# Attention scores' maxima written to SBUF, filler paced by the share of attention work done, and one more gate pair in the quad stage

## The chip, the cores and the metric

The kernel runs on one core of one Trainium2 chip. The metric is device time in microseconds, as the median of the runs. A core has five engines that work side by side from their own queues: TensorE (PE, matrix products), VectorE (DVE), ScalarE (ACT), GpSimd (POOL) and SyncE (SP, which here only issues transfers). PE writes its results to the accumulator memory (PSUM), from which DVE and ACT read; all else lives in SBUF or in device memory.

## The reference

One layer of a streaming encoder, on a prompt of 1024 rows and a sample of 64 rows, all of width 1024 and in float32. One input projection gives nine groups of columns:

```python
xn = rms_norm(x, g_pre)
z = xn @ w_in
xa, ga, q, k, v, gb, fl, ma, mb = jnp.split(z, np.cumsum(sizes)[:-1], axis=-1)
```

Branch A is a causal convolution and a gated linear recurrence over `xa`, times silu(`ga`). Branch B is softmax attention with 16 heads of 64, whose logits carry running sums of log forget gates:

```python
s = jnp.einsum('qhd,khd->hqk', q, k) * (HEAD_DIM ** -0.5)
s = s + cq.T[:, :, None] - ck.T[:, None, :]
s = jnp.where(mask[None], s, -jnp.inf)
p = jax.nn.softmax(s, axis=-1)
return jnp.einsum('hqk,khd->qhd', p, v)
```

times silu(`gb`). Each branch is projected, weighted by sigmoid(`ma`) or sigmoid(`mb`), and the sum goes through one output projection, a norm, the residual and a small gated projection of a per-layer input. The sample attends to a cache of 128 keys beside its own.

## The kernel before, in words

All matrix operands are split in a high and a low part (`xh`, `xl`, `wh`, `wl`), and each product is made of three matmuls: high by high, high by low, low by high. The sequence of the stages is: the projection of `v` (to 123 us), two plain gate panels (to 147 us), the quad stage (to 411 us), attention (to 849 us), branch A's recurrence with its own panels (to about 1030 us), the branch projections, the output projection, and the last gated projection.

**Panels and quads.** A panel is 128 columns of `w_in` times all 1088 rows of `x`: three chunks of 364, 364 and 360 rows, eight steps of `k` each, three matmuls a step (`panel_steps`, L172 to L174; 72 matmuls). A quad is a pair of such panels made by seven half-size products instead of eight (`seven`, `product`, L818): 7 products of 4 `k` steps, 3 matmuls, 2 halves of 272 rows; 168 matmuls. The list `quads` holds the keys and queries, then `xa` and early `ga` columns, then `MORE` pairs of gate columns that are taken from the end of the list `gates`. What is left in `gates` are the panels that serve as filler in attention. The results of gate panels and quads are parked in device memory (`d_ma`, `d_mb`, `d_gb`, `d_ga`).

**Attention.** A unit is one head and one block of 256 queries (64 units, in the order of blocks 0, 3, 1, 2 in each head). Its steps are: `s`, the scores of 128 queries into one of two accumulator tiles, `s1` (up to 512 keys) or `s2` (up to 1024), one of each; `softmax`, which on DVE adds the mask and takes the row's maximum (L1143), on ACT takes the exponential with row sums (L1145), on DVE the reciprocal (L1147) and on POOL the normalisation (L1148) of the SBUF tile `pr` (named `pb` or `pm` in the trace); `t`, three or four transposes of `pr` on PE (L1185), whose result ACT and DVE split in `th` and `tl` (L83, L86); and `v`, four matmuls with the values (L1213, L1215), which end with a copy `lo` on ACT and a sum `y` on DVE. The sample's steps are `sk`, `ss`, `st` and `sv`. POOL makes the values' high and low halves `vv` (L1109, L86) from transfers that SP issues (`load_v`).

**What sets the order.** The order on PE, ACT, DVE and POOL in attention is written by a planner while the kernel is built. It keeps a clock `now` that moves by the cost of each matmul group, and `book` puts the work of the other engines in their calendars at the costs of the constants at the top (`D_MAX`, `A_EXP`, `G_NORM` and so on). `ready` tells when the next step of each of the three queues may start by this calendar: for `s`, when the accumulator tile is free (`s_free`); for `t`, when both normalisations and a transpose tile are done; for `v`, when `tl` is. The main loop takes the first queue whose step has been ready for `SLACK` = 600 ns; if there is none it takes one filler step (3 matmuls of a gate panel), and only when there is no filler left does it wait for the earliest step. A finished filler chunk is copied out of the accumulator by ACT (`st`); the weights of the next filler panel are split on ACT and DVE (`book_split`). The transfers for head 0 and its values are issued when the stage begins.

After attention, `recur_in(1)` takes the first panel of branch A (72 matmuls, beginning at L172 with the tag `acc`), while ACT and DVE make the convolution of the first 128 channels, which the matmuls `gacc` need after 96 further matmuls. `split_next` splits the next panel with two copies on ACT (`wh`, `wl`) and an adding transfer.

Of the kernel before, what the change touches and what calls it, by code (L numbers as in the profile page):

```python
# [9 lines left out]
AF = mybir.ActivationFunctionType  # L10
ALU = mybir.AluOpType
# [3 lines left out]
D = 1024  # L15
KT = D // P
# [10 lines left out]
NEG = -1e30  # L27
# [5 lines left out]
CW = HT // 2  # L33
PLAIN = 2

MORE = 2
W_SC = 1092
GC = 364

HOP_PE, HOP, SLACK = 250.0, 90.0, 600.0  # L40
D_MAX, D_INV, D_LO, D_Y, D_YS = (310.0, 1.035), 160.0, (130.0, 1.1), 420.0, 230.0
A_EXP, A_HI, A_LO, A_ST, A_W = (450.0, 0.85), (150.0, 0.88), 380.0, 470.0, 1060.0
G_NORM = (260.0, 0.84)
# [23 lines left out]
def hybrid_step(tc, a, o):  # L67
# [939 lines left out]
    def book(engine, at, ns, do=None):  # L1007

        busy = booked[engine]
        while busy and busy[0][1] < now[0] - 20000.0:  # L1010
            busy.pop(0)
        i = 0
        while i < len(busy) and busy[i][0] < at + ns:
            at = max(at, busy[i][1])
            i += 1
        busy.insert(i, (at, at + ns))
        if do is not None:
            serial[0] += 1
            heapq.heappush(agenda, (at, serial[0], do))
        return at + ns + HOP  # L1020
# [6 lines left out]
    def per(cost, n):  # L1027
        return cost[0] + cost[1] * n
# [67 lines left out]
    def load_v(p, i, tag="v_raw"):  # L1096

        raw = p2.tile([P, SEQ if tag == "pb" else SEQ // 2], F32, name=tag, tag=tag, bufs=4 if tag == "pb" else 1)
        raw = raw[:, :SEQ // 2].rearrange("q (b d) -> q b d", d=P)
        b = slice(4 * i, 4 * i + 4)  # L1100
        sp.dma_start(raw, o["v_prompt"][i * SEQ // 2:(i + 1) * SEQ // 2, p * P:(p + 1) * P].rearrange(
            "(b q) d -> q b d", q=P))
        for j in range(2):
            if i == 0:
                heads_v[2 * p + j] = p2.tile([P, NBLK, 2, HD], F32R, name="vv", tag="vv", bufs=3)
            vv = heads_v[2 * p + j]
            src = raw[:, :, j * HD:(j + 1) * HD]
            at = now[0] + 8000.0 + 3000.0 * j
            at = book("G", at, 360.0, lambda vv=vv, src=src: pool.tensor_copy(vv[:, b, 0, :], src))  # L1109

            def low(vv=vv, src=src):
                sub(pool, vv[:, b, 1, :], src, f(vv[:, b, 0, :]))
                n_halves[0] += p == 0

            book("G", at, 740.0, low)
# [6 lines left out]
    def load_sample(p):  # L1122
        cols = slice(p * P, (p + 1) * P)
        t = {n: p2.tile(s, F32, name=n, tag=n, bufs=1) for n, s in (("kc", [P, P]), ("vc", [P, P]), ("vn", [DEC, P]))}
        sp.dma_start(t["kc"][:, :], a["cache_k"][:, cols])
        sp.dma_start(t["vc"][:, :], a["cache_v"][:, cols])
        sp.dma_start(t["vn"][:, :], o["v_sample"][:, cols])
        sp.dma_start(f(cs_k[2:, :]), d_cs[2 * p:2 * p + 2].rearrange("h s t -> (h s) t"))
        sp.dma_start(f(cs_q[:2, :]).rearrange("s (h t) -> s h t", h=2), d_cq[:, 2 * p:2 * p + 2, :])
        t["ks"] = [p2.tile([P, LS], F32R, name=f"ks{i}", tag=f"ks{i}", bufs=1) for i in "hl"]  # L1130
        for i in range(2):
            sp.dma_start(f(t["ks"][i][:, PAST:]), d_k[i, p][:, SEQ:])
            for j in range(2):
                js = slice(j * HD, (j + 1) * HD)
                sp.dma_start(f(qs[i][js, js]), d_q[i, p][js, SEQ:])
        smp[p] = t
        smp_at[p] = now[0] + (12000.0 if p else 24000.0)

    def softmax(s, n, pr, m):


        nm, sm = (p2.tile([P, 1], F32, name=x, tag=x, bufs=8)[:, :] for x in ("nm", "sm"))
        at = book("D", now[0] + HOP_PE, per(D_MAX, n), lambda: dve.tensor_tensor_reduce(  # L1143
            out=s[:, :n], in0=s[:, :n], in1=m, scale=-1.0, scalar=-NEG, op0=ALU.add, op1=ALU.min, accum_out=nm))
        free = book("A", at, per(A_EXP, n), lambda: act.activation(  # L1145
            out=pr[:, :n], in_=s[:, :n], func=AF.Exp, scale=-1.0, bias=nm, accum_out=sm))
        at = book("D", free, D_INV, lambda: dve.reciprocal(out=sm, in_=sm))  # L1147
        return free, book("G", at, per(G_NORM, n), lambda: pool.tensor_scalar(  # L1148
            out=pr[:, :n], in0=pr[:, :n], scalar1=sm, scalar2=1.0, op0=ALU.mult, op1=ALU.mult))

# [216 lines left out]
    load_v(0, 0)  # L1367
    load_v(0, 1, "pb")
    load_sample(0)
    fill = filler()  # L1370
    while s_q or t_q or v_q:
        catch_up()
        times = [(i, ready(q[0])) for i, q in enumerate((s_q, t_q, v_q)) if q]
        times = [(i, at) for i, at in times if at is not None]
        best = next((i for i, at in times if at + SLACK <= now[0]), None)
        if best is None:
            if next(fill, False):
                continue
            at, best = min((at, i) for i, at in times)
            now[0] = max(now[0], at)  # L1380
            catch_up()
        go((s_q, t_q, v_q)[best].popleft())
    while next(fill, False):
        catch_up()
    catch_up(float("inf"))
# [872 lines left out]
```

## Time and profile before

| what | us |
|---|---|
| median of 3 runs (lowest, highest) | 1454.27 (1453.98, 1455.23) |
| the profiled execution, whole | 1453.95 |
| its span, first to last instruction | 1452.0 |
| around the span | 1.95 |
| PE busy | 1429.0 |
| DVE, ACT, POOL busy | 898.5, 715.5, 317.3 |

In the profile a matmul's row shows its start and a modelled length that overlaps the next one's: matmuls of 364 columns start 0.166 us apart and are shown as 0.33 us long. So what a group of matmuls costs is read from the starts of the first and of the row behind the last, and a wait of PE costs the shown idle time and the part of the length that would have overlapped, some 0.16 us more.

### The profile page before, as it was taken

The page shows a single profiled execution, that of the slowest core. Times are in us where ns is not written, and L with a number is a line of the kernel's source. Part 1 is how long each engine was busy: PE and PEld are TensorE (multiplying, and loading weights), DVE is VectorE, ACT ScalarE, POOL GpSimd, SP SyncE. Part 2 cuts the span into 40 slices and gives each one's busy share as a digit, 9 for nine tenths or more (in the row PEclk, how much of TensorE's full clock was granted, in tenths as well). Part 3 has the DMA queues.
Part 4 walks back from the last instruction along what each step waited for, and adds up shares of the span by engine and source line. Part 5 has one row for each costly group of instructions (what it writes and reads, how often), then busy time and mean ns, then how long its engine had stood idle before and what let it go on. Part 6 is the DMA issues. An engine that isn't in the chain of part 4 may idle for free.

```text
span 1452.0 us, 25721 instructions
## 1 busy us (share of the span) xinstructions
PE 1429.0 (98%) x9653; PEld 1388.6 (96%) x9653; DVE 898.5 (62%) x1640; ACT 715.5 (49%) x1353; POOL 317.3 (22%) x449
## 2 busy tenths in 40 slices
PE   8999999999999999999999999999999999999997
PEld 8999999999999999999999989999999999879997
DVE  5554765664325666666566555898747565788544
ACT  5423534442225566666555656777535233554533
POOL 0012333323223443444333310221011000000001
PEclk9999999999999999999999999999999999999999
DMA  6767556754276665646545344454178775134101
GB/s 220 214 129 109 150 159 176 189 181 114 83 204 162 121 148 140 139 115 140 124 128 137 57 109 73 89 94 83 65 264 306 264 216 176 58 107 157 48 34 44
DMA packets 143544, 200.64 MB, mean 138 GB/s; under 512 B 24212, under 2 KB 106620, under 8 KB 142396
## 3 DMA queue, kind: packets, MB, share of 16 engines
q1 hardware_dynamic: 126316, 162.61, 43.5%
q0 software_dynamic: 6336, 19.67, 4.9%
q10 hardware_dynamic: 10768, 16.73, 3.2%
q8 instruction: 76, 1.25, 0.3%
q14 instruction: 48, 0.39, 0.1%
HBM read 131.04 MB, written 65.80 MB: 136 GB/s over the span
## 4 chain that ended last, share of the span: by engine, by line
PE 82%; DVE 7%; DMA 4%; ACT 3%; issue 2%; POOL 1%; SPq 0%; DVEq 0%; ACTq 0%; POOLq 0%
PE quad L818 17%; PE acc L174 11%; PE acc L172 11%; PE acc L173 11%; PE tp L1185 4%; PE q L1905 4%; PE pv L1213 2%; PE pv L1215 2%; PE s L1163 2%; PE s L1164 2%; PE vacc L172 2%; PE vacc L173 1%; PE vacc L174 1%; DMA d_mix<-st_a 1%; DMA d_y<-y 1%
## 5 line engine op out<-in xcount | busy, mean ns | idle before, releaser
L172 PE MATMUL acc<-xh,wh 128*128 128x364 f32 (+1 forms) x768 | 252.5, 329 | 0.2 <-ACT st L83 0.2
L173 PE MATMUL acc<-xl,wh 128*128 128x364 f32 (+1 forms) x768 | 251.6, 328 | 0.0
L174 PE MATMUL acc<-xh,wl 128*128 128x364 f32 (+1 forms) x768 | 251.4, 327 | 0.0
L172 PEld LDWEIGHTS acc<-xh,wh 128*128 128x128 f32 x768 | 144.5, 188 | 1.2 <-ACT st L83 0.5
L173 PEld LDWEIGHTS acc<-xl,wh 128*128 128x128 f32 x768 | 144.3, 188 | 0.5
L174 PEld LDWEIGHTS acc<-xh,wl 128*128 128x128 f32 x768 | 144.1, 188 | 0.0
L1143 DVE CUSTOM_DVE_ANT_0 s<-s,mask 128x1024 f32<-128x1024 f32 (+7 forms) x128 | 95.5, 767 | 30.0 <-PE s L1164 29.7
L86 DVE TENSOR_TENSOR wl<-w_raw,wh 128x1024 fp32r<-128x1024 f32 (+1 forms) x53 | 60.1, 1135 | 71.5 <-ACT wh L83 68.1
L83 ACT ACTIVATE wh<-w_raw 128x1024 fp32r<-128x1024 f32 (+1 forms) x65 | 63.3, 975 | 82.9 <-PE quad L818 30.0
L1148 POOL TENSOR_SCALAR pb<-pb,sm 128x896 f32<-128x896 f32 (+1 forms) x64 | 61.7, 963 | 139.9 <-DVE sm L1147 120.3
L86 DVE TENSOR_TENSOR tl<-tp,th 128x512 fp32r<-128x512 f32 x96 | 65.8, 689 | 29.2 <-ACT th L83 29.1
L818 PE MATMUL quad<-xh,wh 128*128 128x272 f32 x384 | 80.7, 291 | 0.0
L818 PE MATMUL quad<-xl,wh 128*128 128x272 f32 x384 | 79.5, 288 | 0.0
L818 PE MATMUL quad<-xh,wl 128*128 128x272 f32 x384 | 79.4, 288 | 0.0
L83 ACT ACTIVATE th<-tp 128x512 fp32r<-128x512 f32 x96 | 57.0, 597 | 37.8 <-PE tp L1185 37.5
L1145 ACT ACTIVATE pb<-s,nm 128x896 f32<-128x896 f32 (+1 forms) x64 | 61.1, 955 | 26.0 <-DVE nm L1143 25.1
L1163 PE MATMUL s<-k,q 128*128 128x256 f32 (+1 forms) x192 | 67.1, 353 | 0.2 <-ACT pb L1145 0.2
L1164 PE MATMUL s<-k,q 68*128 68x256 f32 (+1 forms) x192 | 65.0, 350 | 0.0
L1185 PE MATMUL tp<-ident,pb 128*128 128x128 f32 x416 | 63.7, 274 | 1.2 <-DVE diag0l L86 0.7
L173 PE MATMUL acc<-ybl,wh 128*128 128x364 f32 (+1 forms) x192 | 62.9, 328 | 0.0
L174 PE MATMUL acc<-ybh,wl 128*128 128x364 f32 (+1 forms) x192 | 62.8, 327 | 0.0
L172 PE MATMUL acc<-ybh,wh 128*128 128x364 f32 (+1 forms) x192 | 62.6, 326 | 0.0
(718 smaller groups left out, 4167.4 us busy)
## 6 DMA issues: line engine op xcount, KB each, us to landing
w_raw<-in_w_in SPq DMA_DIRECT2D x56, 256.0 KB
q<-d_q SPq DMA_DIRECT2D x48, 256.0 KB
k<-d_k SPq DMA_DIRECT2D x48, 256.0 KB
w_raw<-in_w_in SPq DMA_DIRECT2D x64, 128.0 KB
w_raw<-in_w_branch SPq DMA_DIRECT2D x32, 256.0 KB
wl<-w_raw POOLq DMA_DIRECT2D x12, 512.0 KB, 4.6
wraw<-in_w_in SPq DMA_DIRECT2D x20, 256.0 KB
d_k<-oh ACTq DMA_DIRECT2D x16, 272.0 KB
```

The costliest lines, as they stand in the source:

```text
L83: return act.activation(out=out, in_=in_, func=AF.Copy, scale=scale)
L86: return eng.tensor_tensor(out=out, in0=in0, in1=in1, op=ALU.subtract)
L172: pe.matmul(out, ah, bh, start=start, stop=False)
L173: pe.matmul(out, ah, bl, start=False, stop=False)
L174: pe.matmul(out, al, bh, start=False, stop=stop)
L818: pe.matmul(acc[:, c, :CW], l[:, k, :], r[:, k, c * CW:(c + 1) * CW], start=(first and k == 0 and p == 0), stop=(k == 3 and p == 2), skip_ ...
L1143: at = book("D", now[0] + HOP_PE, per(D_MAX, n), lambda: dve.tensor_tensor_reduce(out=s[:, :n], in0=s[:, :n], in1=m, scale=-1.0, scalar=-N ...
L1145: free = book("A", at, per(A_EXP, n), lambda: act.activation(out=pr[:, :n], in_=s[:, :n], func=AF.Exp, scale=-1.0, bias=nm, accum_out=sm))
L1148: return free, book("G", at, per(G_NORM, n), lambda: pool.tensor_scalar(out=pr[:, :n], in0=pr[:, :n], scalar1=sm, scalar2=1.0, op0=ALU.mul ...
L1163: pe.matmul(s[:, c0:c0 + w], t["q1"][:, q0:q0 + P], t["k1"][:, c0:c0 + w], start=True, stop=False)
L1164: pe.matmul(s[:, c0:c0 + w], t["q2"][:HD + 4, q0:q0 + P], t["k2"][:HD + 4, c0:c0 + w], start=False, stop=True)
L1185: pe.transpose(tp[:, o0 + i * P:o0 + (i + 1) * P], pr[par][:, kb * P:(kb + 1) * P], ident[:, :])
```

## The change

Four things are changed.

1. `softmax` writes the masked scores into the SBUF tile `pr` instead of back into the accumulator tile, and the exponential runs in place in `pr`. The accumulator tile counts as free when DVE has taken the maximum, no longer when ACT has taken the exponential.
2. The main loop counts the attention work done so far (`own`, by `own_time`) and the filler steps used (`filled`). Where the next step isn't ready for 600 ns, filler is taken only up to the same share of filler as of own work; beyond it, the step that is ready first goes ahead if it has been ready for `LEAST` = 300 ns.
3. The first head's value halves are booked on POOL 20 us after the stage begins, no longer 8 us.
4. `MORE` is 3: one more pair of `gb` panels (columns 256 to 511) is made as a quad, and attention has 360 filler steps instead of 408.

```diff
-MORE = 2
+MORE = 3
...
-HOP_PE, HOP, SLACK = 250.0, 90.0, 600.0
+HOP_PE, HOP, SLACK, LEAST = 250.0, 90.0, 600.0, 300.0
...
-            at = now[0] + 8000.0 + 3000.0 * j
+            at = now[0] + (8000.0 if p else 20000.0) + 3000.0 * j
...
         at = book("D", now[0] + HOP_PE, per(D_MAX, n), lambda: dve.tensor_tensor_reduce(
-            out=s[:, :n], in0=s[:, :n], in1=m, scale=-1.0, scalar=-NEG, op0=ALU.add, op1=ALU.min, accum_out=nm))
-        free = book("A", at, per(A_EXP, n), lambda: act.activation(
-            out=pr[:, :n], in_=s[:, :n], func=AF.Exp, scale=-1.0, bias=nm, accum_out=sm))
-        at = book("D", free, D_INV, lambda: dve.reciprocal(out=sm, in_=sm))
+            out=pr[:, :n], in0=s[:, :n], in1=m, scale=-1.0, scalar=-NEG, op0=ALU.add, op1=ALU.min, accum_out=nm))
+        free = at
+        at = book("A", at, per(A_EXP, n), lambda: act.activation(
+            out=pr[:, :n], in_=pr[:, :n], func=AF.Exp, scale=-1.0, bias=nm, accum_out=sm))
+        at = book("D", at, D_INV, lambda: dve.reciprocal(out=sm, in_=sm))
...
+    def own_time(step):
+
+        kind, x, i = step
+        if kind == "s":
+            full = 256 * (units[x][1] + 1)
+            return sum(2 * (0.44 * min(512, full - c0) + 8) for c0 in range(0, full, 512))
+        if kind == "t":
+            return 109.0 * (3 if i == units[x][1] else 4)
+        return {"v": 480.0, "sk": 109.0, "ss": 440.0, "st": 218.0, "sv": 840.0}[kind]
+
     fill = filler()
+    own_total = sum(own_time(step) for q in (s_q, t_q, v_q) for step in q)
+    own = 0.0
+    filled = 0
+    n_fill = 3 * KT * (1 + sum(e[0][0] == "r" for e in ahead) + sum(len(g[1]) for g in gates))
     while s_q or t_q or v_q:
         catch_up()
         times = [(i, ready(q[0])) for i, q in enumerate((s_q, t_q, v_q)) if q]
         times = [(i, at) for i, at in times if at is not None]
         best = next((i for i, at in times if at + SLACK <= now[0]), None)
         if best is None:
-            if next(fill, False):
+            at, first_ = min((at, i) for i, at in times) if times else (now[0] + 1e9, None)
+            over = filled >= n_fill * own / own_total
+            if not (over and at + LEAST <= now[0]) and next(fill, False):
+                filled += 1
                 continue
-            at, best = min((at, i) for i, at in times)
+            best = first_
             now[0] = max(now[0], at)
             catch_up()
-        go((s_q, t_q, v_q)[best].popleft())
+        step = (s_q, t_q, v_q)[best].popleft()
+        own += own_time(step)
+        go(step)
```

How the planner's order moves is seen at three places. Lines of the changed kernel behind the softmax are one higher than before (L1186 is the transposes' line).

**POOL, where attention begins.** `vv` are the first head's value halves, made from the transferred `v_raw` and `pb`; `pm` and `pb` with `sm` are the normalisations of the first units. Before:

```order
L1109 CAST vv<-v_raw 128x4x64
L86 TENSOR_TENSOR vv<-v_raw,vv 128x4x64
L1109 CAST vv<-pb 128x4x64
L86 TENSOR_TENSOR vv<-pb,vv 128x4x64
L1088 DMA d_ma<-st 128x364
L1148 TENSOR_SCALAR pm<-pm,sm 128x128
L1088 DMA d_ma<-st 128x364
L1148 TENSOR_SCALAR pb<-pb,sm 128x896
L1148 TENSOR_SCALAR pm<-pm,sm 128x256
```

Of the change:

```order
L86 TENSOR_TENSOR vv<-v_raw,vv 128x4x64
L1109 CAST vv<-pb 128x4x64
L86 TENSOR_TENSOR vv<-pb,vv 128x4x64
L1149 TENSOR_SCALAR pm<-pm,sm 128x128
L1109 CAST vv<-v_raw 128x4x64
L86 TENSOR_TENSOR vv<-v_raw,vv 128x4x64
L1109 CAST vv<-pb 128x4x64
L86 TENSOR_TENSOR vv<-pb,vv 128x4x64
L1149 TENSOR_SCALAR pb<-pb,sm 128x896
L1149 TENSOR_SCALAR pm<-pm,sm 128x256
```

The first normalisation now stands between the halves of the first and of the second head, no longer behind both, and no filler's outgoing transfer stands between the normalisations.

**PE, at the end of attention.** Before, from the last filler row on, there are scores, transposes and value products alone, down to the first matmul of branch A. Its last rows:

```order
L1185 MATMUL tp_10560<-ident,pb 128x128 x3
L1213 MATMUL pv<-tl,vv 128x256
L1215 MATMUL pv<-th,vv 128x256
L1213 MATMUL pv<-tl,vv 128x256
L1215 MATMUL pv<-th,vv 128x256
L1213 MATMUL pv<-tl,vv 128x256
L1215 MATMUL pv<-th,vv 128x256
L1213 MATMUL pv<-tl,vv 128x256
L1215 MATMUL pv<-th,vv 128x256
L1213 MATMUL pv<-diag0l,vv 128x256
L1215 MATMUL pv<-diag0h,vv 128x256
```

Of the change, with the semaphores that each row waits for; the last row is the first matmul of branch A:

```order
L1216 MATMUL pv<-th,vv 128x256
L172 MATMUL acc<-xh_110,wh 128x360
L173 MATMUL acc<-xl_112,wh 128x360
L174 MATMUL acc<-xh_110,wl 128x360
L1214 MATMUL pv<-diag0l,vv 128x256 [waits DVE_49]
L1216 MATMUL pv<-diag0h,vv 128x256
L1214 MATMUL pv<-diag0l,vv 128x256
L1216 MATMUL pv<-diag0h,vv 128x256
L172 MATMUL acc<-xh_109,wh 128x364 [waits Activation_49]
```

Filler rows stand between the last units down to the last four matmuls of attention, and the first matmul of branch A waits for ACT, which it did not before. What it waits for is the copy `st` of the filler's last chunk, whose accumulator bank it takes.

**ACT, at the same place.** `wh` and `wl` from `w_raw` are the split of branch A's second panel, `st` is that last filler copy, `lo` the last unit's copy, `g_h` and `uh` belong to branch A. Before, `wh`, `st` and `wl` stand some twenty rows earlier, among the last units' exponentials, and the stage ends with:

```order
L83 ACTIVATE lo<-pv 64x256 [waits DVE_49,PE_49]
L83 ACTIVATE th<-tp_10531 128x512 [waits PE_49]
L83 ACTIVATE th<-tp_10545 128x512 [waits DVE_49,PE_49]
L83 ACTIVATE lo<-pv 64x256 [waits DVE_49,PE_49]
L83 ACTIVATE diag0h<-tp_10560 128x384 [waits PE_49]
L83 ACTIVATE lo<-pv 64x256 [waits DVE_49,PE_49]
```

Of the change:

```order
L83 ACTIVATE lo<-pv 64x256 [waits DVE_49,PE_49]
L83 ACTIVATE diag0h<-tp_10596 128x384 [waits PE_49]
L83 ACTIVATE wh<-w_raw 128x1024 [waits DMAHW2_49,DMAHW1_49,DMAHW7_49,DMAHW0_49,PE_49]
L83 ACTIVATE st<-acc 128x360 [waits DMASW5_49,PE_49]
L83 ACTIVATE lo<-pv 64x256 [waits DVE_49,PE_49]
L83 ACTIVATE wl<-wh 128x1024 [waits Activation_49]
L83 ACTIVATE g_h<-st 128x256 [waits DMAHW5_49,DMAHW3_49,DMAHW6_49,DMAHW2_49,Pool_49]
```

The split of the second panel now stands ahead of the copy that branch A's first matmul waits for.

## The prediction

> **What bounds the kernel now.** I read the page's list of engines first, then busy times by stage, then PE's waits and its timeline where the waits lie.
>
> ```profile
> PE 1429.0 (98%) x9653; PEld 1388.6 (96%) x9653; DVE 898.5 (62%) x1640; ACT 715.5 (49%) x1353; POOL 317.3 (22%) x449
> ```
>
> PE is busy for 98% of the span, so a change is worth only what it takes from PE's work or from its few waits. By stage (columns: length, then busy time and instructions of PE, PE's weight loads, DVE, ACT, POOL; granted clock, transfer share, GB/s):
>
> ```profile
> 146.87:390.42 243.55, 243.55 (x1949) 242.62 (x1949) 144.98 (x217) 95.38 (x176) 78.08 (x58) 1.00 0.53 151
> 390.42:411.50 21.08, 21.08 (x171) 21.08 (x170) 6.08 (x8) 2.89 (x5) 6.36 (x15) 1.00 0.69 209
> 411.50:831.86 420.36, 418.57 (x2820) 403.07 (x2819) 253.52 (x650) 240.72 (x566) 159.46 (x245) 1.00 0.58 132
> 831.86:849.05 17.19, 13.80 (x95) 11.48 (x95) 10.42 (x23) 11.45 (x23) 4.60 (x10) 1.00 0.58 119
> ```
>
> The first two are eleven quads and the last one, without a gap on PE. The third is attention as long as there is filler: 1.79 us idle in 420. The fourth is the end of attention, after the last filler row, and there PE stands idle for 3.39 us of 17.19. DVE and ACT are busy for 57 to 60% of attention, so neither is the bound. PE's waits, first from 440 to 831.8 us and then from 831.8 to 849.1 us:
>
> ```profile
> PE pv L1213 <- ACT lo L83: 0.4, 2, 0.2
> ```
>
> ```profile
> PE tp L1185 <- DVE tl L86: 1.2, 2, 0.8
> PE tp L1185 <- DVE diag0l L86: 0.7, 1, 0.7
> PE pv L1213 <- DVE y L1224: 0.6, 1, 0.6
> PE pv L1213 <- ACT lo L83: 0.5, 1, 0.5
> PE s L1163 <- ACT pb L1145: 0.2, 1, 0.2
> ```
>
> While filler lasts, two waits of 0.2 us are all that 390 us show. Without it, the short chain score, maximum, exponential, normalisation, transpose, split, values is laid bare.
>
> **The pair as a quad.** PE's timeline at the last quad, at the first filler panel, and at one more place:
>
> ```profile
> 390.42 0.41 PE L818 MATMUL quad<-xh,wh 128*128 128x272 f32 x2
> ...
> 411.50 0.33 PE L172 MATMUL acc<-xh,wh 128*128 128x364 f32 x1
> ...
> 423.40 0.33 PE L172 MATMUL acc<-xh,wh 128*128 128x364 f32 x1
> ...
> 437.49 0.32 PE L174 MATMUL acc<-xh,wl 128*128 128x360 f32 x1
> 439.14 0.55 PE L1185 MATMUL tp<-ident,pm 128*128 128x128 f32 x3 [1.34 <-POOL pm L1148]
> ```
>
> From 411.50 to 423.40 runs one panel of 72 matmuls: 11.90 us, two of them 23.80. The last quad, a gate pair too, takes 21.08 (390.42 to 411.50). The thirteenth costs the same, and its sums and splits lie beside PE (DVE 6.08 and ACT 2.89 of 21.08). So this gives -2.72. If it cost the mean of the eleven, 243.55/11 = 22.14 with the keys' transposes, which a gate pair doesn't have, it would give -1.66; I take -2.72, by the row that is of its kind. Its weights are now loaded in the place of `w_raw`, and the first filler's load waits behind their split; but on SP that load already stands behind the quad's last results, so nothing is later.
>
> **The first value halves.** The wait at 439.14 is POOL's. POOL's timeline:
>
> ```profile
> 431.20 0.40 POOL L1109 CAST vv<-v_raw 128x256 fp32r<-128x256 f32 x1 [24.95 <-DMA v_raw<-out_v_prompt]
> ...
> 436.65 0.39 POOL L1148 TENSOR_SCALAR pm<-pm,sm 128x128 f32<-128x128 f32 x1
> ```
>
> The halves stand ahead of the normalisations in the queue, although their data lands only at 431.2, and four pairs of them keep POOL until 436.65. In the new order the first normalisation follows the second pair, the other two follow the fourth, and two outgoing transfers are gone from ahead of and between them. So they end sooner, and the wait goes: 439.14 - 437.49 - 0.16 = 1.49 us (bounds -1.49, and 0 if the transposes should move forward by as much). Values aren't needed before the transposes, so the later halves delay nothing.
>
> **Filler to the end.** What would the end of attention cost without waits? Counts and pace:
>
> ```profile
> L1185 PE MATMUL tp<-ident,pb 128*128 128x128 f32 x26 | 4.2, 279 | 1.2 <-DVE diag0l L86 0.7 <-DVE tl L86 0.4
> L1185 PE MATMUL tp<-ident,pm 128*128 128x128 f32 x10 | 1.6, 274 | 0.8 <-DVE tl L86 0.8
> L1163 PE MATMUL s<-k,q 128*128 128x512 f32 x3 | 1.3, 428 | 0.2 <-ACT pb L1145 0.2
> L1163 PE MATMUL s<-k,q 128*128 128x256 f32 x2 | 0.6, 283 | 0.0
> ```
>
> ```profile
> 833.04 0.49 PE L1185 MATMUL tp<-ident,pm 128*128 128x128 f32 x3
> ...
> 833.84 0.60 PE L1185 MATMUL tp<-ident,pb 128*128 128x128 f32 x4
> ...
> 834.63 0.28 PE L1215 MATMUL pv<-diag2h,vv 128*128 128x256 f32 x1
> ```
>
> The first three score pairs (512, 256 and 512 keys) run from 831.86 to 833.04, 1.18 us; the other two (512 and 256) then take 1.18 x 768/1280 = 0.71. Three transposes with four value matmuls take 0.80, four with four 0.91 (833.84 to 834.63, and 0.12 for the last). There are 36 transposes (six groups of four, four of three), five score pairs, and, of the 95 matmuls, 95 - 1 - 36 - 10 = 48 for values, two groups of four without transposes. Work: 6 x 0.91 + 4 x 0.80 + 2 x 0.48 + 1.18 + 0.71 = 11.5. The stretch takes 17.19, so its waits cost 5.7; I enter -5.6. The lower bound is the shown idle time with 0.16 for each of the six listed waits: 4.4. The new order keeps filler between the units down to the last four matmuls, so each of these steps finds its data older.
>
> **A new wait.** The last filler chunk is now finished 0.65 us ahead of the end of attention (three matmuls' last at 0.166, then four of 0.12), and its copy `st` stands on ACT behind the split `wh`. What that pair takes is shown where it stood before:
>
> ```profile
> 831.90 1.06 ACT L83 ACTIVATE wh<-w_raw 128x1024 fp32r<-128x1024 f32 x1 [1.17 <-PE acc L173]
> 832.86 0.45 ACT L83 ACTIVATE st<-acc 128x360 f32<-128x360 f32 x1
> ```
>
> From the start of `wh` to the end of `st` it is 1.41 us. `wh` starts when L173, the last matmul but one, has ended (0.33 us after its start, which is 0.65 + 0.166 ahead of the end), some 0.45 us ahead of the end, so branch A's first matmul waits 1.0 us, and all of PE's queue behind it. Bounds: 0 (if `wh` waited less) and 1.4. The matmuls `gacc` stand 96 places behind; their operands come later too, since the last `lo` is late and two small loads now stand ahead of the convolution's input on SP:
>
> ```profile
> 832.12 1.13 SPq L1426 DMA_DIRECT2D st<-in_w_rg_a  x2
> ```
>
> ```profile
> 861.07 1.30 DVE L86 TENSOR_TENSOR ul<-u,uh 128x1092 fp32r<-128x1092 f32 x1 [0.85 <-ACT uh L83]
> ```
>
> ```profile
> 864.97 0.33 PE L172 MATMUL gacc<-uh,g_h 128*128 128x364 f32 x1
> ```
>
> `ul` ends at 862.37, so 2.6 us are spare; 1.13 for the loads and about 0.5 for `lo` fit in. If that cover were gone, each microsecond over would be one on PE.
>
> **The softmax and the thinner slack.** The accumulator tile is free one exponential sooner, which lets scores be placed earlier; it removes no work. Prices of the pieces in attention:
>
> ```profile
> L1143 DVE CUSTOM_DVE_ANT_0 s<-s,mask 128x1024 f32<-128x1024 f32 x16 | 19.7, 1230 | 7.4 <-PE s L1164 7.4
> ```
>
> ```profile
> L1145 ACT ACTIVATE pb<-s,nm 128x1024 f32<-128x1024 f32 x16 | 17.9, 1116 | 2.4 <-DVE nm L1143 1.7 <-DVE sm L1147 0.7
> ```
>
> and in the quad stage, ACT's copies of one size from SBUF (`ko`) and from the accumulator (`quad`):
>
> ```profile
> L83 ACT ACTIVATE oh<-ko 128x544 fp32r<-128x544 f32 x32 | 20.9, 654 | 16.9 <-DVE ko L849 16.6
> L83 ACT ACTIVATE ko<-quad 128x544 f32<-128x544 f32 x12 | 7.3, 611 | 0.0
> ```
>
> The planner's price for the maximum at 1024, 310 + 1.035 x 1024 = 1370, covers the measured 1230 and the reading of the result behind it; for the exponential, 450 + 0.85 x 1024 = 1320 stands over 1116. So 300 ns of its slack are about 300 real ones. The maximum has the same operands and writes elsewhere; the trace shows no such form, and I take no difference (40 ns either way, as ACT's pair differs, is off PE's path). The exponential from SBUF may cost 654 - 611 = 43 ns more, 136 times 5.8 us of ACT, which has 180 us idle; it makes normalised rows 43 ns later against 300 of slack. I take 0 for it, with 5.8 as the price if every one were exposed.
>
> [...]
>
> Steps that now go ahead at 300 ns, not 600, may meet late data. In the bare end of attention six waits cost 5.6, 0.9 each; I enter one such, +0.9 (bounds 0, and 3.7 for four).
>
> **The sum**, against the profiled execution (1453.95; the span is 1452.0): -2.72 - 1.49 - 5.6 + 1.0 + 0.9 = -7.9, so 1446.0. The median of the runs shown stands 0.32 above the profiled one: 1446.4. The likeliest case's own range is 1444.5 (neither of the two costs) to 1448.6 (the smaller gains of quad and end).
>
> **Rivals.** *All covers hold*: no wait at branch A, none from thin slack: -9.8, so 1444.5. For it speaks the quiet middle of the stage; against it ACT's order, `wh` ahead of `st`. Chance 0.17. *Slack given back*: ten waits of 0.4 us, as half of the bare ones: -8.8 + 4, so 1449.5. For it: more filler-poor stretches, as 48 filler steps are gone; against: planned and measured prices agree. Chance 0.15. *No spread*: the end keeps its waits, since the last steps hang on one chain, and quad and start alone gain: -4.2, so 1450.1. The order's filler rows speak against it. Chance 0.05. *Exponential exposed*: each unit waits for its 43 ns: -7.9 + 5.8, so 1452.2, no change that can be told. Against it: transposes stand a filler step or more behind. Chance 0.05. *Slower*: thin slack as a rule: the bare end lost 5.6 us over some 24 steps, 0.23 each; from 38 such steps of the stage's 450 on the gain of 8.8 is eaten, and at one in each of 64 units it is -8.8 + 14.7, so 1460.2. The two waits in 390 us speak against it. Chance 0.04.
>
> **How the numbers follow.** The forecast has 0.54. About 0.2%, 2.9 us, is what a measurement of this kernel can tell from no change. Forecast, first, second and third rival lie below 1451.4 (together 0.91); for the edges of the last two I give 0.03 away: faster 0.88, same 0.08, slower 0.04. The range, 1443.4 to 1450.6, takes in the first four cases, with a microsecond below the lowest of them, about the spread of the runs shown (1453.98 to 1455.23).
>
> **What would show it.** Right: thirteen quads at 21.1 us; no wait on `pm` near 439; attention's last stretch without idle time of PE; one wait of the first `acc` behind attention for ACT's `st`, near 1 us; `gacc` without one. Wrong: a dozen waits of `tp` or `s` spread over the stage (the slack), or a gap ahead of `gacc`.

## The result: slower by 0.35%

The changed kernel takes 1459.21 us (median of 8 runs, 1457.96 to 1460.65) against 1454.45 us of the kernel before beside it. The ratio is 1.0035, with a 95% interval of 1.0025 to 1.0044: slower by 3.6 to 6.4 us, where -7.9 was forecast. Its profiled execution has a span of 1458.7 us, 6.7 above that of before. The medians are 4.8 apart: the profiled execution of the changed kernel, at 1460.57, was one of the slower of its eight, and the accounts by stages below are of it.

The page's list of engines for the changed kernel:

```profile
PE 1430.1 (98%) x9677; PEld 1388.2 (95%) x9677; DVE 898.3 (62%) x1649; ACT 723.9 (50%) x1353; POOL 318.7 (22%) x445
```

PE is as busy as before (1429.0), although work was taken from it. The stages tell where the time lies: quads, attention, branch A to its last panel of the recurrence, the projections, the rest (columns as in the prediction). Before:

```profile
146.87:411.50 264.63, 264.63 (x2118) 263.69 (x2118) 151.06 (x225) 98.27 (x181) 84.44 (x73) 1.00 0.54 156
411.50:849.05 437.55, 432.38 (x2914) 414.56 (x2913) 263.94 (x673) 252.17 (x589) 164.06 (x254) 1.00 0.58 131
849.05:1028.54 179.49, 179.29 (x1083) 178.98 (x1081) 132.89 (x138) 122.62 (x178) 31.13 (x66) 1.00 0.43 84
1028.54:1221.92 193.38, 191.73 (x1154) 191.09 (x1154) 120.65 (x184) 66.88 (x82) 15.82 (x29) 1.00 0.64 215
1221.92:1452.00 230.08, 219.00 (x1499) 201.96 (x1498) 149.93 (x275) 116.26 (x211) 3.83 (x4) 0.99 0.26 90
```

The changed kernel:

```profile
146.84:432.75 285.91, 285.81 (x2285) 284.77 (x2285) 160.75 (x236) 103.24 (x189) 89.76 (x77) 1.00 0.53 152
432.75:852.88 420.13, 410.80 (x2770) 392.26 (x2768) 253.74 (x671) 254.69 (x581) 157.78 (x240) 0.99 0.58 127
852.88:1033.70 180.82, 179.71 (x1081) 178.96 (x1082) 133.85 (x139) 124.58 (x180) 33.01 (x72) 1.00 0.48 93
1033.70:1229.50 195.80, 193.48 (x1154) 192.58 (x1154) 119.78 (x183) 65.96 (x81) 15.81 (x29) 0.99 0.63 213
1229.50:1458.70 229.20, 218.83 (x1499) 201.94 (x1498) 150.16 (x275) 116.19 (x211) 3.83 (x4) 0.99 0.26 90
```

The quads cost 21.28 us more, as forecast (21.08). Attention is 17.42 shorter, where the terms add up to 28.99 (-23.80 - 1.49 - 5.6 + 1.0 + 0.9): 11.6 are missing. Another 1.3 were lost in branch A and 2.4 in the projections, stages that the change doesn't touch; 0.9 came back at the end. PE's waits name the places:

```profile
PE pv L1214 <- DVE y L1225: 6.3, 2, 5.8
PE acc L174 <- DVE wl L86: 2.1, 1, 2.1
PE s L1165 <- DMA k<-d_k: 1.2, 1, 1.2
PE acc L172 <- ACT st L83: 1.1, 2, 0.9
PE gacc L173 <- DVE ul L86: 0.9, 1, 0.9
```

The waits of the bare end of attention and the one for `pm` are gone, and the new one for `st` is there, all as forecast. What the forecast didn't have is the first line: one wait of 5.84 us in the middle of attention, at 749.8.

**What PE waits for there.** PE's timeline at the place, then that of DVE:

```profile
749.55 0.27 PE L1238 MATMUL tps<-ident,kc 128*128 128x128 f32 x1
755.66 0.58 PE L1214 MATMUL pv<-tl,vv 128*128 128x256 f32 x1 [5.84 <-DVE y L1225]
756.04 0.41 PE L1216 MATMUL pv<-th,vv 128*128 128x256 f32 x1
```

```profile
755.19 0.42 DVE L1225 TENSOR_TENSOR y<-pv,lo 64x256 f32<-64x256 f32 x1 [6.54 <-DMA d_y<-y]
```

DVE can't write the sum `y` of a unit, because the tile (one of three) still holds the sum of three units earlier: its store into `d_y` hasn't landed. PE's next value matmul waits for this sum itself, which reads the accumulator `pv` that the matmul writes: it starts at 755.66, when `y` (755.19 and 0.42) has just ended. The store stands on SP. SP's timeline:

```profile
731.70 2.30 SPq L257 DMA_DIRECT2D w_raw<-in_w_in  x4
734.10 4.56 SPq L1038 DMA_DIRECT2D q<-d_q  x2
738.70 3.88 SPq L1038 DMA_DIRECT2D k<-d_k  x2
742.67 1.23 SPq L1038 DMA_DIRECT2D q<-d_q  x1
...
746.57 0.28 SPq L1040 DMA_DIRECT2D q<-d_rows  x1
747.61 0.47 SPq L1201 DMA_DIRECT2D d_y<-y  x1
```

SP waits 5.4 us for a weight split of DVE before it issues the next weights (1 MB, at 731.7). Then it issues the eight loads of a head behind them, and slowly: from 734.10 to 746.57, the last of them held for the weights' landing, and only at 747.61 the store of a sum that DVE had made at 735.0. By the trace's semaphores the weights land at 746.6, the store at 755.07. In the kernel before, the same weights went out at 684.2, with no head's loads behind them, and at 731.5 the head's loads and the store went ahead of the next weights:

```profile
684.20 2.56 SPq L257 DMA_DIRECT2D w_raw<-in_w_in  x4
687.88 1.33 SPq L1101 DMA_DIRECT2D v_raw<-out_v_prompt  x1
689.25 8.22 SPq L1200 DMA_DIRECT2D d_y<-y  x3
...
731.47 1.09 SPq L1038 DMA_DIRECT2D q<-d_q  x2
...
736.08 0.47 SPq L1200 DMA_DIRECT2D d_y<-y  x1
736.75 3.22 SPq L257 DMA_DIRECT2D w_raw<-in_w_in  x4
```

The wait has a second price. The granted clock around it, in the view by stretches:

```profile
749.60:753.00 3.40, 0.22 (x2) 0.00 (x0) 0.00 (x0) 0.44 (x2) 0.34 (x1) 1.00 1.03 254
753.00:759.83 6.83, 4.17 (x16) 3.93 (x16) 1.08 (x3) 0.47 (x1) 2.19 (x4) 0.50 0.34 85
759.83:763.24 3.41, 3.41 (x25) 3.23 (x25) 1.66 (x6) 1.51 (x6) 0.43 (x1) 1.00 0.21 57
```

From 753.00 to 759.83 PE has half its clock. From the first matmul behind the wait to the one of `cs_k` it takes 4.18 us (755.66 to 759.84); the same matmuls take 2.30 in a kernel without the wait (`y_pool` below, 750.45 to 752.75). So the place costs 5.84 + 0.16 + 1.9 = 7.9 us. The wait for `wl` in the projections, 2.11 us where it was 1.44, is followed by 3.41 us at half clock too (1097.75 to 1101.16). `y_pool` below has the same wait without it and is 1.7 us shorter there.

### The profile page after: what moved, and what is told of

Its sections match the earlier page's. It is cut to its first block, busy times and chain, and to the rows that moved or that the text cites. A ratio compares the mean times of both kernels' runs of the same rounds, so it can differ in the third digit from the quotient of the medians.

```text
span 1458.7 us, 25782 instructions
## 1 busy us (share of the span) xinstructions
PE 1430.1 (98%) x9677; PEld 1388.2 (95%) x9677; DVE 898.3 (62%) x1649; ACT 723.9 (50%) x1353; POOL 318.7 (22%) x445
## 4 chain that ended last, share of the span: by engine, by line
PE 81%; DMA 6%; DVE 6%; ACT 3%; issue 2%; SPq 1%; DVEq 0%; ACTq 0%; POOL 0%; POOLq 0%
PE quad L818 18%; PE acc L172 10%; PE acc L174 10%; PE acc L173 10%; PE q L1925 5%; PE tp L1186 4%; PE pv L1214 3%; PE pv L1216 3%; PE s L1165 2%; PE s L1164 2%; PE vacc L172 1%; PE vacc L173 1%; PE vacc L174 1%; DMA w_raw<-in_w_in 1%; DMA wl<-w_raw 1%
## 5 line engine op out<-in xcount | busy, mean ns | idle before, releaser
L172 PE MATMUL acc<-xh,wh 128*128 128x364 f32 x720 | 237.8, 330 | 1.1 <-ACT st L83 1.1
L173 PE MATMUL acc<-xl,wh 128*128 128x364 f32 x720 | 236.1, 328 | 0.0
L174 PE MATMUL acc<-xh,wl 128*128 128x364 f32 x720 | 236.1, 328 | 0.0
L172 PEld LDWEIGHTS acc<-xh,wh 128*128 128x128 f32 x720 | 135.6, 188 | 3.0 <-ACT st L83 1.6
L1146 ACT ACTIVATE pb<-pb,nm 128x896 f32<-128x896 f32 (+1 forms) x64 | 63.2, 987 | 21.5 <-DVE nm L1143 16.2
L1143 DVE CUSTOM_DVE_ANT_0 pb<-s,mask 128x896 f32<-128x896 f32 (+1 forms) x64 | 64.8, 1012 | 3.4 <-PE s L1165 3.3
L818 PEld LDWEIGHTS quad<-xh,wh 128*128 128x128 f32 x416 | 65.4, 188 | 0.2
L818 PEld LDWEIGHTS quad<-xh,wl 128*128 128x128 f32 x416 | 65.5, 188 | 0.0
L818 PEld LDWEIGHTS quad<-xl,wh 128*128 128x128 f32 x416 | 65.4, 188 | 0.0
L1214 PE MATMUL pv<-tl,vv 128*128 128x256 f32 x192 | 56.5, 317 | 7.2 <-DVE y L1225 6.3
```

Source lines behind the costliest of these rows:

```text
L172: pe.matmul(out, ah, bh, start=start, stop=False)
L173: pe.matmul(out, ah, bl, start=False, stop=False)
L174: pe.matmul(out, al, bh, start=False, stop=stop)
L818: pe.matmul(acc[:, c, :CW], l[:, k, :], r[:, k, c * CW:(c + 1) * CW], start=(first and k == 0 and p == 0), stop=(k == 3 and p == 2), skip_ ...
L1146: at = book("A", at, per(A_EXP, n), lambda: act.activation(out=pr[:, :n], in_=pr[:, :n], func=AF.Exp, scale=-1.0, bias=nm, accum_out=sm))
L1214: pe.matmul(pv[:, :256], v, tl[:, c], start=(g == 0 and j == 0), stop=False)
```

## Experiments

The experiments' numbers are medians of five runs or more, each beside the kernel before (1453.1 to 1453.8 there). Two theories were open at first: that SP's order did it, or that the transfer engines were simply full.

**The stores of y leave SP.**

```diff
-            sp.dma_start(dst, y[:, :])
+            pool.dma_start(dst, y[:, :])
...
-            leave(1)
+            leave(0)
```

> The changed kernel, with the 64 stores of y into d_y issued by POOL, right behind the sum that makes y, and no longer by SP one unit later; the order on PE, DVE and ACT is untouched. Theory (the store stands on SP behind loads that wait for other engines and for the 1 MB weight load): PE's wait of 5.84 us at 749.8 goes, and with it the 6.83 us of half granted clock from 753.0: -5.84 - 0.16 - 3.4 = -9.4, from 1459.2 to 1449.8 (1448.5 to 1451). Rival A (the 16 transfer engines are full there, so that a store from any queue lands late): a wait of 4 us or more stays near 750, 1457 to 1460. Rival B (POOL's 64 new issues of 0.54 us make the normalisations late): the wait goes, but waits of transposes for pm and pb are spread over attention, 1452 to 1456.

Measured 1448.63 (1448.31 to 1449.40), 0.9964 of before with an interval of 0.9952 to 0.9977: faster than both kernels. POOL's issue of the same sum's store, and PE at the place:

```profile
735.92 0.58 POOL L1201 DMA_DIRECT2D d_y<-y  x1 [2.59 <-DVE sm L1148]
```

```profile
750.45 0.39 PE L1214 MATMUL pv<-tl,vv 128*128 128x256 f32 x1 [0.46 <-DVE y L1225]
```

Issued at 735.92, 11.7 us earlier, the store lands at 747.59. It takes 11.7 us to land (the median of POOL's stores there is 3.1, the longest 12.1), longer than the one in the changed kernel (7.5): the transfer engines are indeed full (a busy share of 0.99 to 1.05 from 735 to 750 in the changed kernel), but that alone isn't too late. The place in SP's order is the cause. The edit does two things at once, another queue and an issue one unit sooner; the next sum is made only 3.1 us later (738.17), so the rest of the 11.7 us is SP's queue, but neither half was run alone. Rival B fell too; no wait for `pm` or `pb` appears. The gain is 10.6 and not 9.4, for reasons I had not expected: by stages of the profiles, which are 11.8 apart, attention gives 7.2 (I had put the half clock at 3.4; it costs 1.9), branch A 1.4, the projections 1.7 (no half clock behind the same wait of 2.11) and the end 1.6.

**The same on the kernel before** (same edit).

> The kernel before, with nothing changed but the 64 stores of y, which POOL issues right behind the sum that makes y. Theory (the cause is what the change made of SP's order; before, DVE's y waited for such a store once, 1.4 us, and PE hardly): no difference, 1453.8 within 0.7. Rival (SP's queue held y up before as well, so that the way out by POOL is a gain of its own, and not a repair of the change): 1452 or less.

1455.10, ratio 1.0009 (1.0000 to 1.0017). Attention takes 437.31 us, as before (437.55): there the stores on SP cost nothing, and it is the change that made them matter. Which of its four parts did, no run isolates; the thirteenth quad alone (`quad_alone` below) has no such wait, while `rows_first` and `st_first`, which keep the new order, have it at 5.31 and 5.85 us. The total isn't quite "no difference": the end is 2.1 shorter and the projections 5.7 longer, with waits of 3.2 and 2.1 us for `wl`, which I didn't follow up.

**Head 0's load at 451.**

```diff
+        rows = (("k2", 0), ("q2", 2))
+        for n, j in rows if h == 0 else (): sp.dma_start(f(t[n][HD:HD + 4, :]), d_rows[h, j:j + 4, :])
         for name, d, i, r in (("q1", d_q, 0, 0), ("q1", d_q, 1, HD), ("k1", d_k, 0, 0), ("k1", d_k, 0, HD),
...
-        sp.dma_start(f(t["k2"][HD:HD + 4, :]), d_rows[h, 0:4, :])
-        sp.dma_start(f(t["q2"][HD:HD + 4, :]), d_rows[h, 2:6, :])
+        for n, j in rows if h else (): sp.dma_start(f(t[n][HD:HD + 4, :]), d_rows[h, j:j + 4, :])
```

> The changed kernel, with head 0's two small loads from d_rows issued ahead of its six large ones, no longer behind them; nothing else moves. Theory (the second d_rows load was issued at 449.5 us only, 4.0 us late, because on SP it waited for one of the filler's outgoing transfers d_ma, which since the value halves were put off go out on ACT's queue): PE's wait of 1.18 us at 451.4 goes, -1.3, from 1459.2 to 1457.9. Rival (the load that stands last waits for that transfer, whichever it is, and PE for it): the wait stays at 1 us or more on a large load, 1459.2 within 0.5.

1460.51 (ratio 1.0046, 1.0033 to 1.0058): the rival, though above its number.

```profile
453.08 0.36 PE L1165 MATMUL s<-k,q 68*128 68x256 f32 x1 [1.90 <-DMA d_ma<-st]
```

The wait grew to 1.90 us, and 3.41 us at half clock follow it (453.32 to 456.73). What is last lands late here too: by the semaphores it is now the last large `k`, at 452.99, and the row names an earlier transfer of the same semaphore.

**The copy ahead of the split** at the end of attention.

```diff
-            halves_of[:] = [copy_act(wh[:, :, :], raw)]
+            with tc.issue_after(last_st.pop().ins) if last_st else contextlib.nullcontext(): halves_of[:] = [copy_act(wh[:, :, :], raw)]
```

> The changed kernel, with the last filler copy st ahead of the split wh on ACT at the end of attention; these two rows change places, nothing else. Theory (branch A's first matmul waits for st behind wh): PE's wait of 0.87 us at 852 falls to 0.2 or less, and ACT's lo, the last y and the loads behind it on SP come no later, so the wait of gacc near 869 stays at 0.9: -0.7, from 1459.2 to 1458.5. Rival (gacc's time is set by the loads of xp, which do not move, so what the first wait loses the second gains): the wait of gacc grows to 1.6, 1459.2 within 0.4.

1457.51 (ratio 1.0026, 1.0016 to 1.0036). Branch A's first matmul no longer waits, and `gacc` still does, 0.89 us, as the theory had it. One more microsecond than expected went; it fits that in this profile the wait for `wl` (2.02 us) is followed by no half clock.

**One more quad alone.**

```diff
-MORE = 2
+MORE = 3
```

> The kernel before with MORE = 3 and nothing else: 360 filler steps, taken as greedily as before. Theory (without the pacing the filler just ends sooner): the stretch without filler at the end of attention grows from 17 us by about 48/408 of 420 us less the 24 us of the filler itself, to some 40 us, with its waits at the same share (5.7 of 17.2), so 7 us more of them: -2.7 + 7 = +4, 1454.4 to 1458.5 (1456 to 1462). Rival (the term of the prediction stands by itself): -2.7, 1451.7 within 0.7. In both the thirteenth quad takes 21.1 us.

1463.16 (ratio 1.0064, 1.0050 to 1.0077), +9.3, worse than either number. The last 59 us of attention:

```profile
800.00:858.89 58.89, 49.38 (x320) 40.79 (x319) 41.22 (x110) 39.30 (x93) 22.92 (x37) 1.00 0.38 80
```

PE is idle for 9.5 of them. Without the pacing, filler that is gone is missed where there is none. The first wait for `pm` is 1.99 us here, and behind it the clock is half for 3.41 us. The pacing by itself, and `LEAST` at 450 or 600, have no run here.

**The softmax as it was**, on `y_pool`.

```diff
-            out=pr[:, :n], in0=s[:, :n], in1=m, ...
-        free = at
-        at = book("A", at, per(A_EXP, n), lambda: act.activation(
-            out=pr[:, :n], in_=pr[:, :n], ...
+            out=s[:, :n], in0=s[:, :n], in1=m, ...
+        free = book("A", at, per(A_EXP, n), lambda: act.activation(
+            out=pr[:, :n], in_=s[:, :n], ...
```

> The kernel y_pool with the softmax as it was before: masked scores back into the accumulator tile, which is free only when the exponential has been taken. By the term of the prediction (a tile that is free sooner removes no work: 0, and 5.8 us of ACT beside PE the other way): 1448.6 within 1. Rival (the tile sets when scores can be placed, and with the filler paced and 48 steps fewer nothing is left to fill with: the planned stalls at the end of attention rise from 0.0 to 9.8 us): 1456 to 1460.

1452.36 (ratio 0.9992, 0.9983 to 1.0001), between the two: the tile that is free sooner is worth 3.7 us, 3.05 of them in attention (415.99 against 412.94). That is a net number: `y_pool` has waits of 1.30 and 0.87 us that this order hasn't, and this one has six between 825 and 848. In the last 29.54 us of attention PE is idle for 4.99 us here, 1.05 in `y_pool` and 3.39 in the kernel before:

```profile
820.00:849.54 29.54, 24.55 (x165) 20.68 (x163) 19.82 (x51) 20.27 (x46) 12.97 (x20) 1.00 0.50 115
```

**Twelve quads**, on `y_pool`.

```diff
-MORE = 3
+MORE = 2
```

> The kernel y_pool with MORE = 2, so 408 filler steps and twelve quads; softmax, pacing and value halves as in the change. By the term of the prediction (a quad for two panels is worth 2.72): 1451.3 within 0.7. Rival (48 more filler steps between the units cover more of what is late, so the quad is worth less): 1449 to 1450.5. Against 1454.3 of before it tells what pacing, softmax and halves bring together: by the prediction 5.2 to 7.1.

1447.62 (ratio 0.9957, 0.9945 to 0.9970), below `y_pool`: neither number. Here head 0's load is in time, and the wait for `wl` is 1.03 us, so the comparison is one of waits. Two kernels below are without most of them.

**Filler out by POOL from the start** (and `st` first), on `y_pool`.

```diff
-                late = n_halves[0] == 4
+                late = True
```

> The kernel y_pool with two more edits: st ahead of wh on ACT as in st_first, and the first filler chunks go out on POOL as the later ones do, no longer on ACT's queue; the order on PE and DVE is that of y_pool. Theory (head 0's last load waits for one of these four transfers d_ma): PE's waits of 1.30 us at 451.5 and 0.87 us at 844.9 go, -1.4 and -0.9, from 1448.6 to 1446.3 (1445.5 to 1447). Rival (the load is late because the transfer engines are busy with the value halves and the weights, whatever queue the chunks take): the wait at 451 stays above 0.8, 1447.3 to 1448; or POOL's four new issues make the first normalisation pm late, and a wait of 1 us or more for pm is there instead, 1447.5 to 1449.

1449.71 (1447.55 to 1450.72; ratio 0.9968, 0.9957 to 0.9980), above every number given. Head 0's last small load is now issued at 444.3, no longer at 449.5, and PE still waits 1.05 us. By the trace's semaphores the last large `k` lands 19.6 us into the stage in both kernels, although it is issued 9.1 or 11.4 us into it. So my theory, that one of the `d_ma` transfers holds it, fell: 1 MB of weights and six loads of 256 KB stand in one queue; in the changed kernel's trace they land in its order, the weights from 438.95 to 444.04 and the six loads from 445.17 to 452.33.

**The value halves early again**, on `y_pool`.

```diff
-            at = now[0] + (8000.0 if p else 20000.0) + 3000.0 * j
+            at = now[0] + 8000.0 + 3000.0 * j
```

> The kernel y_pool with the first head's value halves booked 8 us after the stage begins, as before. By the term of the prediction (the halves stand ahead of the first normalisations on POOL, whose data comes late): a wait of PE for pm near 458 of 1.3 to 2 us comes back, +1.5, from 1448.6 to 1450.1. Rival (the halves only choose which wait is met: with them early the filler's first chunks leave by POOL and head 0's loads land sooner, so that the wait of 1.30 us at 451.5 goes when the one for pm comes): 1448.6 within 0.6.

1450.78 (ratio 0.9982, 0.9973 to 0.9991). A wait of 1.47 us for `pm` at 460.5 is back, the one of 1.26 at 451.8 stays, and attention takes 1.50 us more (414.44 against 412.94). The term stands.

**First scores 1.5 us later** (and `st` first), on `y_pool`; and **twelve quads with `st` first**.

```diff
-        head_at[h] = now[0] + (10000.0 if h else 18000.0)
+        head_at[h] = now[0] + (10000.0 if h else 19500.0)
```

```diff
-MORE = 3
+MORE = 2
...
-            halves_of[:] = [copy_act(wh[:, :, :], raw)]
+            with tc.issue_after(last_st.pop().ins) if last_st else contextlib.nullcontext(): halves_of[:] = [copy_act(wh[:, :, :], raw)]
```

> The kernel y_pool with st ahead of wh on ACT, and head 0's loads counted as landed 19.5 us after the stage begins, no longer 18, so that filler stands where the first score waited. Theory (head 0's last large load lands 19.6 us into the stage in y_pool and 19.8 in the changed kernel, on SP's queue behind 1 MB of weights, whatever semaphore it waits for): the wait of 1.30 us at 451.5 falls under 0.3, that of 0.87 us at 844.9 goes, -1.3 and -0.9, from 1448.6 to 1446.4 (1445.5 to 1447.3). Rival (1.5 us less room brings waits of the same size elsewhere in attention): 1447.3 to 1449.

> The kernel y_pool with MORE = 2 and st ahead of wh on ACT: its wait of 1.47 us before branch A (where pool_no_quad still had it) goes, so -1.3 from 1447.6 to 1446.3 (1445.5 to 1447.3), the same as pool_late_s. Theory (the thirteenth quad is worth nothing here: 21.4 us for it, against 23.1 that attention loses in matmul time and some 2 us that come in waits): within 0.8 of pool_late_s. Rival (the term of the prediction, 2.72, with the waits taken away on both sides): 2 us or more above pool_late_s.

1445.79 (ratio 0.9947, 0.9935 to 0.9960) and 1446.31 (0.9952, 0.9938 to 0.9965). Both as the theories said, but for another reason than mine. Quads, attention and projections, first of `pool_late_s`, then of `pool_12_quads`:

```profile
146.57:432.42 285.85, 285.83 (x2285) 284.77 (x2285) 161.76 (x236) 103.35 (x189) 90.17 (x77) 1.00 0.53 152
432.42:841.62 409.20, 408.06 (x2771) 390.11 (x2769) 253.46 (x671) 251.86 (x580) 194.68 (x303) 1.00 0.56 131
...
1021.05:1216.61 195.56, 193.28 (x1155) 192.62 (x1155) 119.68 (x183) 65.80 (x81) 15.87 (x29) 0.99 0.63 213
```

```profile
146.84:411.84 265.00, 264.87 (x2118) 263.76 (x2117) 152.87 (x225) 98.27 (x181) 83.13 (x73) 1.00 0.55 156
411.84:844.67 432.83, 431.29 (x2915) 414.22 (x2913) 257.08 (x674) 258.76 (x589) 199.10 (x313) 1.00 0.57 130
...
1024.11:1217.18 193.07, 191.74 (x1155) 191.09 (x1154) 120.49 (x184) 66.87 (x82) 15.81 (x29) 1.00 0.64 216
```

Up to branch A, in one profile of each, the thirteenth quad saves 2.78 us (695.05 against 697.83), or 2.1 without a wait of 0.56 + 0.16 that only the second kernel has. The projections then take 2.5 us more, by the wait for `wl` (2.07 against 1.12) and the half clock behind it.

**That wait shortened**, on `pool_late_s`: the second product of one `yb_in`, and the copy of its result, change places with the split and the copy behind them.

```diff
-        dve.tensor_tensor(out=t[:, :], in0=t[:, :], in1=s[:, :], op=ALU.mult)
+        def rest():
+            h, l = yb[k]; dve.tensor_tensor(out=t[:, :], in0=t[:, :], in1=s[:, :], op=ALU.mult)
...
+            if of == 4:
+                with tc.issue_after(halves_of[1].ins):
+                    rests[2]()
             run(panel_steps(mm, *w, ya, evac_a))
-        branch_b(of)
+        rest = branch_b(of)
+        rests[of] = rest
+        if of != 2:
+            rest()
```

> The kernel pool_late_s with two rows exchanged far behind attention, in the first branch's projection: on DVE the split wl of one panel stands ahead of one product yb_in (1.28 us), no longer behind it, and on ACT the copy ybh of that product stands one row later. There PE waits 2.07 us for wl at 1082, and behind it the granted clock is half for 3.41 us (1085.4 to 1088.9). Theory (a wait of PE of some 1.8 us or more that falls into one stretch of 3.41 us costs the half clock of the next): the wait falls to about 0.9, the half clock goes, -1.2 - 1.7 = -2.9, from 1445.8 to 1442.9 (1442 to 1443.8). Rival (the half clock behind a wait has no price of its own, the matmuls there wait for other engines anyway): -1.2, 1444.6 (1444.1 to 1445.3).

1443.63 (1443.19 to 1444.78; ratio 0.9935, 0.9921 to 0.9949): the fastest of all. PE at the wait, in `pool_late_s` and here, and the granted clock of `pool_late_s` in two stretches of 3.41 us:

```profile
1084.06 0.44 PE L174 MATMUL acc<-yah,wl 128*128 128x364 f32 x1 [2.07 <-DVE wl L86]
```

```profile
1082.89 0.44 PE L174 MATMUL acc<-yah,wl 128*128 128x364 f32 x1 [0.60 <-DVE wl L86]
```

```profile
1082.02:1085.43 3.41, 1.37 (x8) 1.38 (x9) 3.41 (x4) 2.11 (x2) 0.48 (x1) 1.00 0.94 291
1085.43:1088.85 3.42, 3.42 (x13) 3.42 (x12) 2.52 (x4) 1.70 (x2) 0.81 (x2) 0.50 0.96 351
```

The projections take 192.53 us, 3.03 less: 1.47 of the wait, and 1.56 that no wait explains. The half clock, gone here, has its own price, and the rival's mechanism fell by the stages. The medians, 2.2 apart where 2.9 and 1.2 were expected, would not have told by themselves.

## Why the prediction was wrong, by its own steps

- **The pair as a quad, -2.72**: the mechanism holds, the size is -2.1 by the profiles of `pool_late_s` and `pool_12_quads` (quads +20.85, attention -22.9 where 23.80 was put in), inside the bounds given. Their medians show 0.5 of it, since the projections took the rest back.
- **The first value halves, -1.49**: right; -1.50 by `pool_halves8`.
- **Filler to the end, -5.6**: the last stretch has no such waits left. In `pool_late_s` attention is 28.35 us shorter than before; 22.9 are the pair, 1.5 the halves, and one thin wait of 0.62 is in it, so 4.6 remain for this term, near its lower bound of 4.4. Whose work it is I had wrong: it hangs on **the softmax**, entered at 0 because it "removes no work". With the pacing but the old softmax (`pool_no_softmax`) the end of attention is idle for 4.99 us, no less than before (3.39, with more filler to use), and attention as a whole is 3.05 longer. What the pacing brings beside it has no run of its own. The price of the softmax was small, as said: a maximum costs 1212 ns (1230 before), and an exponential 26 to 34 ns more at every length, where I had reckoned with up to 43. After, and at 128 columns before and after:

```profile
L1146 ACT ACTIVATE pb<-pb,nm 128x1024 f32<-128x1024 f32 x16 | 18.4, 1147 | 2.2 <-DVE nm L1143 2.1
```

```profile
L1145 ACT ACTIVATE pm<-s,nm 128x128 f32<-128x128 f32 x15 | 5.5, 366 | 0.7 <-DVE sm L1147 0.6
```

```profile
L1146 ACT ACTIVATE pm<-pm,nm 128x128 f32<-128x128 f32 x16 | 6.3, 392 | 3.4 <-DVE nm L1143 3.4
```

- **A new wait, +1.0**: right, 0.87 + 0.16. Its second half was wrong: `gacc` waits 0.90, since the cover of 2.6 us was used up. I had put 1.13 + 0.5 against it. The loads of `xp` are issued 3.0 us into branch A (855.87 after 852.88) and not 1.6, and from there to the first step of `u` it takes 6.9 us and not 4.2: some 4.0 later in all. In `y_pool`, where SP waits for no `y`, they are issued at +0.6, and there is no wait.
- **The thinner slack, +0.9**: right in size; two waits of 0.46 and 0.41 us in attention. That they come of steps taken at 300 ns isn't shown: both are waits of `pv` for `y`.
- **The step that failed** is the one that all of these rest on: the new order was judged on PE, ACT, DVE and POOL, and SP was looked at only at the two ends of attention ("nothing is later", "two small loads"). That in between each step finds "its data older" takes for granted that the tiles are free, and the tile `y` is free only when SP has got round to its store. The rival on the slower side was built on thin slack as a rule, at 0.04, and the "two waits in 390 us" that spoke against it are waits of the old order. One row of the kernel before, in DVE's waits during attention, showed the place:

```profile
DVE y L1224 <- DMA d_y<-y: 1.4, 1, 1.4
```

It stands at 701.5: a store issued at 689.25, behind the same weights, landed at 701.44. There 1.4 us of lateness had cover on PE. In the new order the weights' load, the head's loads and the store met, and the lateness became 6.54. The sum, term by term: missing are +7.9 for this wait with its clock, +1.3 for head 0's load, +1.3 in branch A, +2.4 in the projections, -0.9 at the end: 12.0 of the 14.6 between forecast (1446.0) and profile (1460.57). Of the 2.4 in the projections 1.7 are half clock behind a wait that `y_pool` has at the same length without it: chance, as the section on the hardware shows. Another 1.6 are the two terms that came out smaller (0.6 and 1.0); the last microsecond lies in no place that I can name.
- That the listed gains were real is shown by `pool_late_s`: with the stores off SP, `st` first and the first scores 1.5 us later the change takes 1445.79, where 1446.4 was forecast for it without these repairs. The nearness is in part chance, for the 1446.4 holds 1.9 us of costs that this kernel doesn't have: the gains alone were put at -9.8, and it shows -7.8 against the kernel before beside it (1453.57). By its stages against those of before the end is 2.3 us shorter (227.74 after 230.08) and the projections 2.2 longer, two things outside the terms that cancel.

## What to carry to other kernels

When a change moves work in time, list for every queue, the transfer queue of an otherwise idle engine too, what now stands ahead of each store that frees a tile; a short wait for such a store on an engine with cover is the warning. Judge a reordering by what frees the buffers as well as by what fills them, and don't take the quiet of the old order as evidence for the new one. A wait of PE may cost more than its length, by the clock granted afterwards: here 5.84 us of wait, and 1.9 more at half clock behind it.

## What the hardware showed that I had not expected

**Half clock came in stretches of 3.41 us.** The half clocks read in mid-kernel lasted 3.41 us or, in the changed kernel at 753.00, twice that; from there to the changed kernel's other one (1097.75) it is 344.75 us, 101 times 3.413. The profiles are divided here into such stretches, carried on from the shown clock changes. At the waits read in these runs: where PE was busy for 0.22, 1.30 (both of the changed kernel), 1.31, 1.37, 1.43, 1.46, 1.50 or 1.51 us (`rows_first`) of one stretch, the next had half the clock; where it was busy for 1.69 (`st_first`), 1.76, 1.76, 1.86, 1.97 us (the kernel before, 1088.72 to 1092.13) or more, it had all of it. In the profiles of the kernel before and of the changed one no stretch from 10 to 1440 us speaks against it. A wait of 1.90 us inside one stretch (`rows_first`, 451.18 to 453.08) was followed by half clock, and one of 3.2 us that fell on two (`before_y_pool`, 1077.25 to 1080.45) was not:

```profile
1075.49:1078.90 3.41, 1.76 (x11) 1.46 (x9) 0.36 (x1) 0.36 (x1) 0.00 (x0) 1.00 1.01 404
1078.90:1082.32 3.42, 1.86 (x11) 1.87 (x12) 3.31 (x5) 0.00 (x0) 0.54 (x1) 1.00 0.26 104
1082.32:1085.73 3.41, 3.41 (x22) 3.41 (x21) 2.67 (x4) 2.70 (x3) 0.54 (x1) 1.00 0.72 218
```

**One load, many speeds.** The 1 MB of weights for a pair of panels lands 6.8 to 15.1 us after its first issue, in attention of the kernel before and of the changed one. In both it is the third and the seventh pair that take longest, wherever they stand: 14.8 and 15.1 us before (issued at 498.24 and 684.20), 14.6 and 14.9 in the changed kernel (526.22 and 731.70); the others take at most 10.8. Why, no run here tells. The weights of 731.7, behind which the store stood, are one of the two.

**The end of the kernel.** With the stores of `y` on SP the time from the last output's landing to the end of the span is 2.2 us in the changed kernel and 3.2 in the kernel before. From the end of that output's issue it is 4.2 and 4.9 us there, and 2.7 in `y_pool`, where the stores are on POOL. The cause is open.
